# Eight weight subtracts of a hybrid encoder trunk placed on GpSimd instead of VectorE

## The chip, the cores and the metric

The kernel runs on one core of one Trainium2 chip. The metric is the device time of one execution in microseconds, median of three runs. A core has a matmul engine (TensorE, PE in the rows), a vector engine (VectorE, DVE), an activation engine (ScalarE, ACT), GpSimd (POOL) and SyncE (SP), which here issues every DMA. Each engine works through its own instructions in a fixed order; between engines there are only semaphore waits.

## What is computed

Two post-norm residual layers on 512 tokens of width 1024, in f32. Layer 0 mixes with windowed attention and a state-space model (S5), layer 1 with a matrix-memory LSTM (mLSTM); behind each mixer stand a residual add with a layer norm, a gated FFN with a depthwise convolution of three taps, and a second residual add with a norm.

```python
SEQ, D_MODEL, D_FF, DEPTH = 512, 1024, 2816, 2
for layer in range(DEPTH):
    y = attn_s5_mixer(x, ...) if layer % 2 == 0 else mlstm_mixer(x, ...)
    x = layer_norm(DEEPNORM_ALPHA * x + y, ln_g[layer, 0], ln_b[layer, 0])
    f = conv_ffn(x, ffn_w_up[layer], ffn_conv_w[layer], ffn_conv_b[layer], ffn_w_down[layer])
    x = layer_norm(DEEPNORM_ALPHA * x + f, ln_g[layer, 1], ln_b[layer, 1])

def conv_ffn(x, w_up, conv_w, conv_b, w_down):
    a, g = jnp.split(x @ w_up, 2, axis=-1)
    return (jax.nn.gelu(dwconv3(a, conv_w, conv_b)) * g) @ w_down

def layer_norm(x, g, b):
    mu = x.mean(-1, keepdims=True)
    var = jnp.mean(jnp.square(x - mu), -1, keepdims=True)
    return (x - mu) * lax.rsqrt(var + LN_EPS) * g + b
```

## The kernel before

**Products in two parts.** PE multiplies rounded f32 (fp32r). So each factor is split into a high part (the rounded value) and a low part (what rounding left), and a product is three matmuls: high by high, high by low, low by high (L545 to L547 in `mm3`, L569 in `nat_tile`).

**Weights in units.** All weights come as 192 units of 128x1024 f32, 512 KB each, in the order of their use. `load_unit` handles one: SP issues the DMA into a staging tile `st` (L511; two of them in the pool `wst`), ACT casts it to the high part `wh` (L528), and `wl = st - wh` is the low part (L529), formed on DVE, or on POOL for the units in the set `ON_POOL`. The subtract is the last reader of `st`, so the DMA of the unit two further on waits for it. `wh` and `wl` live in rings (3 tiles in ring A, 5 in ring B); `prefetch` and `get` set how many units are loaded ahead of their use. Units 14 to 16 serve the S5 gate and the first part of the layer-0 output projection, 17 to 19 the rest of it, 20 to 85 the first FFN (FFN0), 118 to 125 the layer-1 output projection, 126 to 191 the second FFN (FFN1).

**Around the start of an FFN.** The work there is the end of an output projection, four norms, and the first products of the FFN, all interleaved:

- `nat_last` goes over the four token tiles. For each it runs the last matmuls of the output projection (L569), then `norm` (`done`). Half way through tiles 2 and 3 PE also transposes tiles 0 and 1 of the normed residual `x` (`transposes`, L623).
- `norm` for one tile: two adds of the residual to the projection (L591, DVE, from PSUM), the mean (L606, DVE), the square (L607, ACT), `lny = (x - mean) * g` (L608, DVE, 128x1024), the variance (L609, DVE), its power -1/2 `lnrs` (L610, POOL, 128x1), and two halves of `x = lny * lnrs + b` (L613, DVE, 128x512 each).
- `transposes` for one tile: two times four matmuls against the identity (L623), a cast to `xh` (L627, ACT), and `xl` = transposed x minus `xh` (L628, DVE, from PSUM).
- `ffn` begins with three units in two halves of 256 token columns: the first half needs only tiles 0 and 1, and the transposes of tiles 2 and 3 stand between its matmuls.

**Ahead of FFN0** stands the S5 gate (`s_glu`): for each of four feature groups PE makes a bank, ACT a tanh `y` (L1234), DVE a product in `y` (L1236), ACT a cast `mh` (L1240), DVE its low part `ml` (L1241). The tile `x` of the residual is loaded by one DMA of 2 MB (L1332); its space was used by an input of the last `y` product, so that DMA waits for the last L1236. The first four units of FFN0 have the names `wl_2654` (unit 20), `wl_2660` (21), `wl_2865` (22), `wl_2871` (23); those of FFN1 are `wl_8019` (126), `wl_8025` (127), `wl_8249` (128), `wl_8255` (129).

**Order.** Up to the S5 gate the order on each engine is set by a planner with a table of biases; from there on, so at both places of this change, by the scheduler of the tile framework, which orders each engine's instructions by its own estimate of their times.

Of the kernel before, what the change touches and what calls it, by code (L numbers as in the profile page):

```python
# [50 lines left out]
_FFN = "AAA" + "BAB" * 20 + "BBB"  # L51
RINGS = "A" * 10 + "XXXX" + "AAA" + "BBB" + _FFN + "VV" + "A" * 30 + "AAA" + "BBBBB" + _FFN

ON_POOL = set(range(96, 118))

VG = 256 + 32

# [391 lines left out]
class Net:  # L449
# [54 lines left out]
    def load_unit(self, parts=None):  # L504
# [12 lines left out]
        hi, lo = parts  # L517
        pool = ENG_W[i] == "g" if self.plan else i in ON_POOL
        eng = nc.gpsimd if pool else nc.vector
# [1273 lines left out]
```

## Time and profile before

| what | value |
|---|---|
| runs | 1277.31, 1279.6 and 1280.5 us; median 1279.6 us |
| the profiled execution | 1281.08 us, its span in the trace 1279.3 us |
| granted PE clock, mean | 0.985 of full speed |
| PE busy | 1245.1 us, 97% of the span |
| DVE busy | 718.8 us, 56% |
| ACT busy | 527.8 us, 41% |
| POOL busy | 138.0 us, 11% |

The span runs from the first to the last record of the trace; the time of the execution is 1.78 us longer. A busy share is that of the whole span. A line of a timeline gives the start, the length, the engine, the line of code, the operation with its output and inputs, and in brackets how long the engine stood idle before it and what released it; neighbours of one kind are joined with a count.

### The profile page before, as it was taken

To read this page: it belongs to the slowest core of one execution; us is meant where nothing else is said; L and a number is where in the kernel's file an instruction comes from. 1 tells how busy PE (TensorE), PEld (TensorE's weight loads), DVE (VectorE), ACT (ScalarE), POOL (GpSimd) and SP (SyncE) were. 2 spreads that over 40 slices of the span, in tenths; PEclk is the share of its full clock that TensorE was granted. 3 is DMA by queue.
4 is the path that set the end of the run, shared out by engine and by line. 5 is a ranking of instruction groups with operands and counts; after the bars stand their busy time and mean duration, and the time that the engine had idled before them with its cause. 6 is when DMAs were issued, how large, how long until landed. Compare 5 with 4: busy or idle time off the path is not lost.

```text
span 1279.3 us, 17610 instructions
## 1 busy us (share of the span) xinstructions
PE 1245.1 (97%) x6878; PEld 1044.2 (82%) x6878; DVE 718.8 (56%) x1398; ACT 527.8 (41%) x900; POOL 138.0 (11%) x139
## 2 busy tenths in 40 slices
PE   7989899999999999999999999999999999999997
PEld 5777787788888888888889898988988888888886
DVE  7998984765442444434675747375864422544415
ACT  5346764353331233322365747453443321333301
POOL 2013520000000000000015344310000000000000
PEclk9988889999999999999999999999999999999999
DMA  8533633453332333323033232323343321433301
GB/s 249 177 112 98 179 104 110 151 167 99 99 99 85 95 117 98 92 72 101 26 117 99 83 99 75 91 66 132 125 139 99 99 90 60 148 99 97 91 27 66
DMA packets 57459, 135.31 MB, mean 106 GB/s; under 512 B 13888, under 2 KB 22928, under 8 KB 56736
## 3 DMA queue, kind: packets, MB, share of 16 engines
q1 hardware_dynamic: 57376, 134.19, 33.7%
q8 instruction: 54, 0.88, 0.3%
q14 instruction: 29, 0.24, 0.1%
HBM read 129.19 MB, written 4.98 MB: 105 GB/s over the span
## 4 chain that ended last, share of the span: by engine, by line
PE 82%; DVE 10%; DMA 4%; issue 3%; ACT 1%; SPq 0%; POOL 0%; DVEq 0%; POOLq 0%; ACTq 0%
PE b L569 22%; PE b L545 17%; PE b L546 17%; PE b L547 17%; PE b L446 3%; DVE t L446 2%; PE b L1557 1%; PE b L1555 1%; DMA zx<-DZ 1%; DMA t<-xT_dram 1%; DVE C L446 1%; DMA st<-w_dram 1%; DMA x<-x_dram 1%; DVE s L446 1%; DVE c L446 1%
## 5 line engine op out<-in xcount | busy, mean ns | idle before, releaser
L546 PE MATMUL b<-xl,wh 128*128 128x512 f32 (+1 forms) x944 | 357.3, 379 | 1.0 <-DVE xl L628 1.0
L545 PE MATMUL b<-xh,wh 128*128 128x512 f32 (+1 forms) x944 | 357.6, 380 | 0.5 <-ACT xh L627 0.5
L547 PE MATMUL b<-xh,wl 128*128 128x512 f32 (+1 forms) x944 | 357.0, 378 | 0.0
L528 ACT CAST wh<-st 128x1024 fp32r<-128x1024 f32 x175 | 183.7, 1051 | 413.3 <-DMA st<-w_dram 141.0
L529 DVE TENSOR_TENSOR wl<-st,wh 128x1024 fp32r<-128x1024 f32 x153 | 188.1, 1231 | 293.4 <-ACT wh L528 289.6
L546 PEld LDWEIGHTS b<-xl,wh 128*128 128x128 f32 x944 | 177.6, 188 | 34.8 <-DVE xl L628 2.1
L547 PEld LDWEIGHTS b<-xh,wl 128*128 128x128 f32 x944 | 177.6, 188 | 33.2
L545 PEld LDWEIGHTS b<-xh,wh 128*128 128x128 f32 x944 | 177.2, 188 | 33.4 <-ACT xh L627 1.0
L569 PE MATMUL b<-wh,hh 128*128 128x512 f32 x352 | 109.3, 390 | 0.0
L569 PE MATMUL b<-wh,hl 128*128 128x512 f32 x352 | 109.2, 389 | 0.0
L569 PE MATMUL b<-wl,hh 128*128 128x512 f32 x352 | 109.2, 389 | 0.0
L610 POOL TENSOR_TENSOR lnrs<-lnsq,mhalf 128x1 f32<-128x1 f32 x16 | 9.7, 604 | 836.1 <-DVE lnsq L609 774.2
L569 PEld LDWEIGHTS b<-wh,hl 128*128 128x128 f32 x352 | 66.1, 188 | 13.8
L569 PEld LDWEIGHTS b<-wl,hh 128*128 128x128 f32 x352 | 66.1, 188 | 13.7
L569 PEld LDWEIGHTS b<-wh,hh 128*128 128x128 f32 x352 | 65.9, 188 | 13.6
L734 DVE TENSOR_TENSOR c<-c,b 128x512 f32<-128x512 f32 x44 | 30.2, 687 | 65.8 <-PE b L547 65.0
L733 ACT ACTIVATE c<-c 128x512 f32<-128x512 f32 x44 | 27.8, 632 | 80.9 <-DVE c L732 80.8
L529 POOL TENSOR_TENSOR wl<-st,wh 128x1024 fp32r<-128x1024 f32 x22 | 52.4, 2388 | 54.2 <-ACT wh L528 51.3
L591 DVE SCALAR_TENSOR_TENSOR x<-x,b 128x512 f32<-128x512 f32 x48 | 31.1, 683 | 43.0 <-PE b L569 39.3
L446 PE MATMUL b<-xh,wh 128*128 128x512 f32 x80 | 33.1, 418 | 8.1 <-ACT xh L446 8.1
L607 ACT ACTIVATE lnjk<-x,lnmu 128x1024 f32<-128x1024 f32 x16 | 18.5, 1154 | 51.0 <-DVE lnmu L606 51.0
L446 ACT ACTIVATE s<-s,m 128x384 f32<-128x384 f32 (+3 forms) x64 | 33.7, 557 | 13.7 <-DVE m L446 13.4
(330 smaller groups left out, 1864.0 us busy)
## 6 DMA issues: line engine op xcount, KB each, us to landing
st<-w_dram SPq DMA_DIRECT2D x192, 512.0 KB, 3.6
tb<-s5bT_dram SPq DMA_DIRECT2D x16, 256.0 KB, 4.4
zx<-DZ SPq DMA_DIRECT2D x16, 256.0 KB, 4.9
lngb<-ln_dram SPq DMA_DIRECT2D x4, 1024.0 KB, 4.7
nb<-DN SPq DMA_DIRECT2D x16, 256.0 KB, 3.5
t<-xT_dram SPq DMA_DIRECT2D x8, 256.0 KB, 5.7
T<-DK SPq DMA_DIRECT2D x32, 64.0 KB, 2.2
x<-x_dram SPq DMA_DIRECT2D x1, 2048.0 KB
```

The source lines that it names most:

```text
L446: getattr(getattr(nc, s.eng), s.name)(*real(s.args), **real(s.kw))
L528: nc.scalar.copy(out=h, in_=x)
L529: eng.tensor_tensor(out=l, in0=x, in1=h.bitcast(F32), op=ALU.subtract)
L545: mm(ps, lhsT=lh, rhs=rh, start=first, stop=False)
L546: mm(ps, lhsT=lh, rhs=rl, start=False, stop=False)
L547: mm(ps, lhsT=ll, rhs=rh, start=False, stop=last)
L569: mm(acc[h], lhsT=hx[:, tok], rhs=wx[:, 512 * h:512 * h + 512], start=a, stop=b)
L591: self.nc.vector.scalar_tensor_tensor(out=xr, in0=xr, scalar=scale, in1=acc[h], op0=ALU.mult, op1=ALU.add, **kw)
L607: nc.scalar.activation(out=jk, in_=x, func=AF.Square, bias=mu, accum_out=sq)
L733: nc.scalar.activation(out=c, in_=c, func=AF.Gelu_apprx_tanh)
L734: nc.vector.tensor_tensor(out=c, in0=c, in1=pg, op=ALU.mult)
L1555: nc.tensor.matmul(pn[:, 0:130], lhsT=Ws[j][:, i - j, :], rhs=va[:, j, h % 2, 0:130], start=j == 0, stop=j == i)
```

## The change

The set of the units whose low part is formed on POOL gets the first four units of each FFN. Nothing else is edited.

```diff
-ON_POOL = set(range(96, 118))
+ON_POOL = set(range(96, 118)) | {20, 21, 22, 23, 126, 127, 128, 129}
```

The scheduler orders the engines anew, and three places are to be seen. In the rows below a name is that of the code with a number for the tile, and the brackets hold the semaphores that an instruction waits for.

**The start of FFN0.** SP, from the weight DMA of unit 21 on; `st_2862` and `st_2868` are units 22 and 23, `st_2874` and `st_3065` units 24 and 25, `x_2622` is the residual, `lngb` the norm's constants:

```order
 L511 DMA st_2657<-w_dram 128x1024 [waits DMAHW7_49,DMAHW5_49,DVE_49]
-L511 DMA st_2862<-w_dram 128x1024 [waits DMAHW6_49,DMAHW0_49,DVE_49]
-L511 DMA st_2868<-w_dram 128x1024 [waits DMAHW7_49,DVE_49]
+L511 DMA st_2862<-w_dram 128x1024 [waits DMAHW6_49,DMAHW0_49,Pool_49]
+L511 DMA st_2868<-w_dram 128x1024 [waits DMAHW7_49,Pool_49]
 L1332 DMA x_2622<-x_dram 128x4096 [waits DMAHW2_49,DVE_49,PE_49]
-L584 DMA lngb_2631<-ln_dram 128x2048 [waits Pool_49]
+L584 DMA lngb_2631<-ln_dram 128x2048
-L511 DMA st_2874<-w_dram 128x1024 [waits DMAHW4_49,DMAHW1_49,DVE_49]
-L511 DMA st_3065<-w_dram 128x1024 [waits DMAHW0_49,DVE_49]
+L511 DMA st_2874<-w_dram 128x1024 [waits DMAHW4_49,DMAHW1_49,Pool_49]
+L511 DMA st_3065<-w_dram 128x1024 [waits DMAHW0_49,Pool_49]
```

The order of these DMAs is as it was; four weight DMAs now wait for POOL instead of DVE, and the load of `x` stands behind two of them. On POOL the four subtracts stand among the powers of the norms:

```order
+L529 TENSOR_TENSOR wl_2654<-st_2651,wh_2653 128x1024 [waits DMAHW6_49,PE_49,Activation_49]
+L529 TENSOR_TENSOR wl_2660<-st_2657,wh_2659 128x1024 [waits PE_49,DMAHW7_49,Activation_49,Pool_49]
+L529 TENSOR_TENSOR wl_2871<-st_2868,wh_2870 128x1024 [waits DMAHW1_49,DVE_49,Activation_49]
+L610 TENSOR_TENSOR lnrs_2690<-lnsq_2689,mhalf_74 128x1 [waits DVE_49,Pool_49]
 L610 TENSOR_TENSOR lnrs_2729<-lnsq_2728,mhalf_74 128x1 [waits DVE_49]
+L529 TENSOR_TENSOR wl_2865<-st_2862,wh_2864 128x1024 [waits DMAHW0_49,Activation_49,Pool_49]
 L610 TENSOR_TENSOR lnrs_2782<-lnsq_2781,mhalf_74 128x1 [waits DVE_49,Pool_49]
```

Three of them are ahead of the power of tile 0, and unit 22 stands between the powers of tiles 1 and 2.

**The norm of tile 2, ahead of the first products of FFN0.** DVE; `lny_2784` belongs to tile 2, `xl_83` is the low part of the transposed x, here of the two halves of tile 1:

```order
 L606 TENSOR_SCALAR lnmu_2780<-lnsm_2779 128x1
 L608 SCALAR_TENSOR_TENSOR lny_2784<-x_2622,lnmu_2780,lngb_2631 128x1024
-L529 TENSOR_TENSOR wl_2865<-st_2862,wh_2864 128x1024
 L609 TENSOR_SCALAR lnsq_2781<-lnsq_2781 128x1
+L613 SCALAR_TENSOR_TENSOR x_2622<-lny_2784,lnrs_2782,lngb_2631 128x512 x2
 L628 TENSOR_TENSOR xl_83<-b_2806,xh_82 128x4x128
-L613 SCALAR_TENSOR_TENSOR x_2622<-lny_2784,lnrs_2782,lngb_2631 128x512 x2
 L628 TENSOR_TENSOR xl_83<-b_2813,xh_82 128x4x128
```

The subtract of unit 22 is gone from DVE, and both halves of tile 2's L613 have moved ahead of the first low part of tile 1.

**The start of FFN1.** POOL; `hrs_7882` is the last power of the mLSTM, `lnrs_8061` and `lnrs_8106` belong to the norms of tiles 0 and 1:

```order
 L1582 TENSOR_TENSOR hrs_7882<-hrs_7882,mhalf_74 128x4 [waits DVE_49,Pool_49]
+L529 TENSOR_TENSOR wl_8019<-st_8016,wh_8018 128x1024 [waits DMAHW2_49,Activation_49]
 L610 TENSOR_TENSOR lnrs_8061<-lnsq_8060,mhalf_74 128x1 [waits DVE_49]
+L529 TENSOR_TENSOR wl_8025<-st_8022,wh_8024 128x1024 [waits DMAHW3_49,Activation_49]
+L529 TENSOR_TENSOR wl_8249<-st_8246,wh_8248 128x1024 [waits DMAHW4_49,Activation_49,Pool_49]
 L610 TENSOR_TENSOR lnrs_8106<-lnsq_8105,mhalf_74 128x1 [waits DVE_49]
+L529 TENSOR_TENSOR wl_8255<-st_8252,wh_8254 128x1024 [waits DMAHW5_49,Activation_49,Pool_49]
```

Unit 126 stands ahead of the power of tile 0, units 127 and 128 right behind it. On DVE the same stretch reads:

```order
 L591 SCALAR_TENSOR_TENSOR x_2622,lnsm_8103<-x_2622,b_7906 128x512
-L529 TENSOR_TENSOR wl_8025<-st_8022,wh_8024 128x1024
 L613 SCALAR_TENSOR_TENSOR x_2622<-lny_8063,lnrs_8061,lngb_7952 128x512 x2
 L606 TENSOR_SCALAR lnmu_8104<-lnsm_8103 128x1
-L529 TENSOR_TENSOR wl_8249<-st_8246,wh_8248 128x1024
 L608 SCALAR_TENSOR_TENSOR lny_8108<-x_2622,lnmu_8104,lngb_7952 128x1024
```

The two subtracts around tile 0's L613 are gone from DVE, and L613 follows the last add of tile 1.

## Rows read from the trace of the kernel before

**Rows 1.** Two stretches: length, busy PE, PEld, DVE, ACT, POOL; clock, DMA, GB/s

```profile
185.00:275.00 90.00, 87.81 (x638) 74.91 (x635) 56.91 (x86) 41.50 (x60) 3.13 (x4) 1.00 0.39 130
880.00:930.00 50.00, 49.76 (x303) 44.16 (x302) 37.03 (x59) 24.29 (x32) 2.18 (x4) 1.00 0.43 140
```

**Rows 2.** Waits of PE, 190 to 275 us: total us, times, longest

```profile
PE b L546 <- DVE xl L628: 1.0, 3, 0.4
...
PE b L569 <- ACT y L1234: 0.3, 1, 0.3
```

**Rows 3.** All instructions of line L529: ns min/median/max, first and last start

```profile
L529 DVE TENSOR_TENSOR wl<-st,wh x153: 1215/1225/2300, 207.9 to 1243.6; 128x1024 fp32r<-128x1024 f32 x153
...
L529 POOL TENSOR_TENSOR wl<-st,wh x22: 2349/2396/2411, 670.1 to 832.4; 128x1024 fp32r<-128x1024 f32 x22
```

**Rows 4.** Timeline of DVE, then of POOL, about 670 us

```profile
670.59 2.48 DVE L1505 TENSOR_TENSOR kl<-c,kh 128x512 fp32r<-128x512 f32 x1 [1.06 <-ACT kh L1504]
...
670.12 2.40 POOL L529 TENSOR_TENSOR wl<-st,wh 128x1024 fp32r<-128x1024 f32 x1 [4.56 <-ACT wh L528]
```

**Rows 5.** Timeline of POOL, then of DVE, about 700 us

```profile
700.16 1.02 POOL L1582 TENSOR_TENSOR hrs<-hrs,mhalf 128x4 f32<-128x4 f32 x1
701.15 2.35 POOL L529 TENSOR_TENSOR wl<-st,wh 128x1024 fp32r<-128x1024 f32 x1
...
701.22 3.13 DVE L1584 TENSOR_SCALAR hn<-hn,hmv,hrs 128x128 f32<-128x128 f32 x4 [1.14 <-POOL hrs L1582]
```

**Rows 6.** Timeline of POOL, then of DVE, about 150 us

```profile
149.47 1.79 POOL L446 TENSOR_TENSOR C<-C,c 128x512 f32<-128x512 f32 x1
...
149.46 0.67 DVE L446 TENSOR_TENSOR ra<-ra,rb 128x512 f32<-128x512 f32 x1
150.05 2.29 DVE L446 TENSOR_TENSOR_SCAN rb<-R,ra 128x512 f32<-128x512 f32 x1
```

**Rows 7.** Start of FFN0, timeline of DVE, then SP, PE, ACT

```profile
218.38 0.69 DVE L1236 SCALAR_TENSOR_TENSOR y<-y,s 128x512 f32<-128x512 f32 x1
...
225.37 0.69 DVE L1236 SCALAR_TENSOR_TENSOR y<-y,t 128x512 f32<-128x512 f32 x1
...
235.47 0.69 DVE L591 SCALAR_TENSOR_TENSOR x<-x,b 128x512 f32<-128x512 f32 x1 [3.76 <-DMA x<-x_dram]
...
248.80 1.28 DVE L608 SCALAR_TENSOR_TENSOR lny<-x,lnmu,lngb 128x1024 f32<-128x1024 f32 x1
...
252.02 1.42 DVE L613 SCALAR_TENSOR_TENSOR x<-lny,lnrs,lngb 128x512 f32<-128x512 f32 x2
...
226.12 1.45 SPq L1332 DMA_DIRECT2D x<-x_dram  x1
...
241.14 1.22 PE L623 MATMUL b<-ident,x 128*128 128x128 f32 x8
...
251.94 0.39 PE L546 MATMUL b<-xl,wh 128*128 128x256 f32 x1 [0.40 <-DVE xl L628]
...
246.49 1.06 ACT L528 CAST wh<-st 128x1024 fp32r<-128x1024 f32 x1 [1.69 <-PE b L569]
```

**Rows 8.** Start of FFN1, timeline of DVE, then POOL and PE

```profile
895.37 1.22 DVE L529 TENSOR_TENSOR wl<-st,wh 128x1024 fp32r<-128x1024 f32 x1
896.51 1.41 DVE L613 SCALAR_TENSOR_TENSOR x<-lny,lnrs,lngb 128x512 f32<-128x512 f32 x2
...
894.93 0.55 POOL L610 TENSOR_TENSOR lnrs<-lnsq,mhalf 128x1 f32<-128x1 f32 x1 [23.82 <-DVE lnsq L609]
...
896.99 0.62 PE L569 MATMUL b<-wh,mh 128*128 128x512 f32 x2
897.45 1.18 PE L623 MATMUL b<-ident,x 128*128 128x128 f32 x8
```

**Rows 9.** Same columns as rows 1, early in the kernel

```profile
46.00:48.00 2.00, 1.10 (x30) 0.99 (x32) 2.00 (x10) 0.96 (x4) 0.00 (x0) 1.00 0.56 115
48.00:54.00 6.00, 5.80 (x34) 4.57 (x31) 5.30 (x20) 0.44 (x1) 0.00 (x0) 0.72 0.74 254
```

## The prediction

> **What bounds the kernel now.** I read first how much of each stretch PE is busy, then what PE waits for there, then the engines' timelines around those waits. PE bounds the kernel: in the stretch around the start of FFN0 it is busy for 87.81 of 90 us, around the start of FFN1 for 49.76 of 50, at full granted clock in both [rows 1]. What it waits for at the start of FFN0 is little: 1.0 us in three waits for `xl`, which DVE makes, and 0.3 us for the tanh of the gate [rows 2]; at FFN1 all idle time is 0.24 us [rows 1]. So all that a relief of DVE can win there is 1.0 + 0.3 + 0.24, about 1.5 us of 1280. The question is what the change may lose: DVE is not spread thin there, it makes the norm that PE's transposes wait for.
>
> **What the edit moves.** Eight subtracts leave DVE, where one takes 1.225 us, and go to POOL, where the same form takes 2.396 [rows 3]: 9.8 us less on DVE, 19.2 us more on POOL, neither of which bounds the kernel over the span. As a count of busy time that costs nothing. Two things give it a price.
>
> First, POOL and DVE hinder each other. A DVE subtract of 128x512 with both inputs in SBUF that begins 0.47 us into a POOL subtract lasts 2.48 us and ends 0.55 us after it [rows 4]; a product of that size and kind takes 0.69 us where POOL is idle (L1236 at 218.38) [rows 7]. So DVE stood still for the rest of the POOL instruction. Second, a POOL subtract that is queued behind a power goes ahead of the DVE work that the power releases: the power ends at 701.18, the subtract begins at 701.15, and DVE's L1584, released by that power, stands 3.13 us for four pieces and ends 0.85 us after the subtract [rows 5]. And where both have work, they take turns: POOL's add at 149.47 waits for DVE's `ra`, then holds up the scan that stands right behind `ra` on DVE, 2.29 us long [rows 6]. Which DVE instructions are exposed follows from the code: L1236, L1241, L608, L613 and L529 read two SBUF operands; L591 and L628 read one from PSUM and I take them as free.
>
> The Trainium skill, Perfetto Trace Analysis, section "Optimizing Scalar/DVE Operations", speaks for such an offload where DVE is saturated and against one between DVE and GpSimd, since these share a port and it "might not help". By its first half the change would win at most the 1.5 us above; rows 4 and 5 side with the second, and the steps below price it.
>
> **Start of FFN0, units 20 and 21: +1.9 us.** Subtract 20 stood on DVE right ahead of the product L1236 at 218.38 [rows 7]. On POOL it begins at about 217.3 and ends at 219.7; the L1236 now stands ahead of it in DVE's queue but is held until 219.65, +1.13 us net. The rest of the gate is a chain DVE, ACT, DVE, so it carries this on. Subtract 21 then runs on POOL from about 225.4 to 227.8 and holds up the last L1236, which ran from 225.37 to 226.06 [rows 7], and would end at 228.4: +2.35. Behind that wait on SP stands the 2 MB load of `x`, issued at 226.12 [rows 7], in the same breath as the weight DMA ahead of it, which now waits for POOL. So the load is issued 2.3 us later. DVE waited 3.76 us for just this load, until 235.47 [rows 7], so nothing hides it. Some comes back, since the next weight DMA (unit 24) also goes later and shares the load's last microseconds less: I take 2.0. PE's transposes of tile 0 stand at 241.14, 1.22 us long for eight [rows 7], right behind the L613 that feeds them, so PE has no slack there: 1.9 us, of which 1.1 show already at the gate. Bounds: 0.8 (the gate's delay hidden by the load's queue, half the load's delay made up) to 2.4.
>
> **Start of FFN0, units 22 and 23: +1.6 us.** Unit 23 falls into the wait for `x`: nothing. Unit 22's cast stands at 246.49 [rows 7], with the shift at 248.4, so its POOL subtract covers about 249.5 to 251.9. L608 of tile 2 stood at 248.80 [rows 7], would be ready at 250.7, and is held until 251.9. From there: 1.28 for L608 (253.2), 0.7 for variance and power (a power alone takes 0.55 [rows 8]; 253.9), 1.42 for L613 of tile 2, which has moved ahead of L628, then 0.68 for L628: `xl` is there at about 255.9. Before, PE's first matmul with it stood at 251.94, after a wait of 0.40 [rows 7]. With PE going on at 256.0 the total shift is 4.1 us; less the other two waits for `xl`, 0.6 us together [rows 2], which fall away since what they wait for now comes sooner after: 3.5, so 1.6 beyond the 1.9. Bounds: 0 (subtract 22 finds L608 already running and DVE's own saving of 1.225 pays for the order) to 2.2.
>
> **Start of FFN1: +3.9 us.** Subtract 126 stood ahead of the first adds of the norm; without its 1.225 us [rows 3] these start up to that much earlier, but then its POOL form holds up L608 for about as long: the power of tile 0 comes 0.2 us earlier, no more. The power of tile 0 stands at 894.93, subtract 127 at 895.37, L613 behind it at 896.51, the transposes at 897.45 [rows 8]. In the new order subtracts 127 and 128 are queued on POOL right behind that power, as in rows 5. The power ends at 895.28, subtract 127 takes 895.25 to 897.6, the first half of L613 897.6 to 898.3, then by turns [rows 6] subtract 128 to 900.6 and the second half of L613 to 901.3. PE reaches the transposes at 896.99 (they stand ahead of these two matmuls now [rows 8]), waits 1.36 for the first four, makes them, and waits 2.55 for the other four: 3.9 us. No wait of before stands behind it that could give anything back [rows 1]. Bounds: 1.6 if either half of L613 goes ahead of the subtract beside it; 3.9 above. I take the upper end, since its order is that of rows 5 and 6.
>
> The Trainium skill, SBUF — State Buffer, section "Who interferes with whom", has the port as a lock held for a whole instruction, by whoever issues first. By that rule too subtract 127 has the port before L613 can ask, and this term is 3.9 and not 1.6; rows 5 agree, since the released L1584 waited.
>
> **The clock: +1.6 us.** PE idles 3.9 of 4.4 us there. In the stretch from 46 to 48 us it was busy for 1.10 of 2 us, and in the 6 us from 48 on the mean granted clock was 0.72 of full speed, that is, it stood on the lower of its two levels for a part of them [rows 9]. With 5.80 busy us in them that cost 5.80 x 0.28 = 1.6 us. I count one such fall, after the wait at FFN1. Bounds: 0 (no fall) to 3.2 (a second one at FFN0, where the idling comes in several pieces).
>
> **Sum.** 1.9 + 1.6 + 3.9 + 1.6 = 9.0 us. The profiled execution took 1281.08 us (1279.3 span and 1.78 around it), 1.5 above the median of the runs; by its own time the sum gives 1290.1, by the median 1288.6. I forecast **1288.6**. Ends of all bounds: 0.8 + 0 + 1.6 + 0 = 2.4 and 2.4 + 2.2 + 3.9 + 3.2 = 11.7, so 1282.0 and 1291.3. About 0.3% (3.8 us) is what a measurement of this kernel can tell from no change.
>
> **Rivals.**
> - *The delays hide (about 1281).* Subtracts and norm fall between each other, because the scheduler's order makes the cast come late or the engines slip past each other; one of the places survives with its lower bound (1.6). For it: half of the terms hang on offsets of under 1 us between a cast and a norm. Against: DVE works nearly without a gap there and the subtracts on POOL stand directly behind what DVE waits for. 26%.
> - *DVE's relief shows (about 1278).* The subtracts find gaps in DVE's exposed work; then DVE's norm chain is 1.2 us shorter per unit, and PE's waits for `xl` and the gate go. This is the other side: it decides at L613 of FFN1, if its halves run before POOL takes up subtract 127, which needs the cast of unit 127 to end 0.1 us or more after the power instead of before it. Its price is bounded by PE's idle time, 1.5 us: 1278.1. It stays within 0.3%. 5%.
> - *The clock falls twice or stays down longer (about 1291).* Both places make PE idle; the sum with 3.2 for the clock and the upper end of the load's delay, 2.4 for 1.9, is 11.1: 1290.7. 17%.
> - *The change doesn't do what it says.* The order shows the eight subtracts on POOL; nothing else hangs on the set. Under 1%, no time of its own.
>
> **Chances.** The forecast, from 1284 to 1289.5: 52%. With the rivals: faster by over 0.3% has 2% (no row carries it; PE has no more than 1.5 us to win), within 0.3% 29% (the first two rivals), slower by over 0.3% 69%. For 8 in 10 the range leaves out the relief and a part of the hidden case below, and what lies over two clock falls above: 1280.8 to 1291.5.
>
> **What would show it.** In the profile after: DVE's L1236 around 218 and 228 us with 2 us and more instead of 0.69; the issue of `x` at about 228.4 and its landing at 237 to 238; a wait of PE for `xl` of 2 us or more near 255; L613 of tile 0 in FFN1 with 4 to 6 us for its two halves instead of 1.41, and PE's transposes there with two waits of 1.4 and 2.5 us; a granted clock under 1.00 behind them. I am wrong if L613 keeps 1.4 us there (POOL took the port later), if `x` lands as before (the load has slack that I don't see), or if the lengths grow but PE's waits don't.

## The result: slower by 0.64%

The changed kernel takes 1288.61 us in the median of five runs (1284.74 to 1289.44); the kernel before, timed beside it, 1277.31 us (1275.93 to 1280.5). The measured ratio is 1.0064 with a 95% interval of 1.0046 to 1.0081, that is +8.2 us (+5.9 to +10.3). The two medians lie further apart, 11.3 us; medians of five runs are that loose, and those of the kernel before in the later measurements, of 26 to 31 runs, are 1279.1 to 1279.6 us. Forecast were 1288.6 us and +9.0.

To see where the time went I divide the span by four instructions that both kernels have: the first tanh of the S5 gate (L1234 on ACT), the first residual add that ends the first half of FFN0 (L591), the last tile's first add in the last norm of FFN0 (L591), and the first residual add that ends the first half of FFN1. Timelines of ACT and DVE, kernel before:

```profile
213.53 0.60 ACT L1234 ACTIVATE y<-b 128x512 f32<-128x512 f32 x1 [4.69 <-PE b L547]
...
415.40 0.69 DVE L591 SCALAR_TENSOR_TENSOR x<-x,b 128x512 f32<-128x512 f32 x1 [0.97 <-PE b L569]
...
617.11 0.69 DVE L591 SCALAR_TENSOR_TENSOR x<-x,b 128x512 f32<-128x512 f32 x1 [0.28 <-PE b L569]
...
1070.92 0.69 DVE L591 SCALAR_TENSOR_TENSOR x<-x,b 128x512 f32<-128x512 f32 x1 [1.04 <-PE b L569]
```

The same four of the kernel after:

```profile
210.31 0.60 ACT L1234 ACTIVATE y<-b 128x512 f32<-128x512 f32 x1 [4.51 <-PE b L547]
...
417.48 0.69 DVE L591 SCALAR_TENSOR_TENSOR x<-x,b 128x512 f32<-128x512 f32 x1 [1.05 <-PE b L569]
...
619.19 0.69 DVE L591 SCALAR_TENSOR_TENSOR x<-x,b 128x512 f32<-128x512 f32 x1 [0.28 <-PE b L569]
...
1078.10 0.69 DVE L591 SCALAR_TENSOR_TENSOR x<-x,b 128x512 f32<-128x512 f32 x1 [0.66 <-PE b L569]
```

The first stretch ("FFN0 stretch" below) takes 201.87 us before and 207.17 after, +5.30. The second takes 201.71 in both. The third ("FFN1 stretch") takes 453.81 and 458.91, +5.10. What lies ahead of the gate was 3.22 us shorter in this execution of the kernel after, and the rest of the span is equal: 5.30 + 5.10 - 3.22 = 7.2, the difference of the two spans (1286.5 and 1279.3). The 3.22 is not the change's: nothing is moved ahead of the gate, and the twelve further profiles below have it between 0.06 and 5.32 us earlier than the kernel before.

The same two stretches as in [rows 1], kernel after (length, busy PE, PEld, DVE, ACT, POOL, granted clock, DMA share, GB/s):

```profile
185.00:275.00 90.00, 84.33 (x536) 71.39 (x535) 52.25 (x75) 36.97 (x54) 12.71 (x8) 0.98 0.37 125
880.00:930.00 50.00, 46.46 (x258) 39.99 (x257) 32.88 (x50) 18.29 (x25) 11.96 (x8) 0.97 0.43 137
```

PE is idle for 5.67 us in the first (2.19 before) and 3.54 in the second (0.24 before), and the mean clock, 1.00 before, is below it in both. What PE waited for, 190 to 275 us (answers [rows 2]):

```profile
PE b L546 <- DVE xl L628: 2.4, 1, 2.4
PE b L623 <- DVE x L613: 1.5, 1, 1.5
PE b L569 <- ACT y L1234: 0.9, 1, 0.9
```

and 880 to 930 us:

```profile
PE b L623 <- DVE x L613: 3.3, 2, 2.1
```

**Start of FFN1.** Timeline of the kernel after, POOL, then DVE, then PE (answers [rows 8]):

```profile
892.66 2.41 POOL L529 TENSOR_TENSOR wl<-st,wh 128x1024 fp32r<-128x1024 f32 x1 [19.50 <-ACT wh L528]
896.90 0.55 POOL L610 TENSOR_TENSOR lnrs<-lnsq,mhalf 128x1 f32<-128x1 f32 x1 [1.83 <-DVE lnsq L609]
897.41 2.39 POOL L529 TENSOR_TENSOR wl<-st,wh 128x1024 fp32r<-128x1024 f32 x1
900.06 2.49 POOL L529 TENSOR_TENSOR wl<-st,wh 128x1024 fp32r<-128x1024 f32 x1 [0.26 <-ACT wh L528]
...
893.28 0.68 DVE L591 SCALAR_TENSOR_TENSOR x<-x,b 128x512 f32<-128x512 f32 x1
...
897.49 5.62 DVE L613 SCALAR_TENSOR_TENSOR x<-lny,lnrs,lngb 128x512 f32<-128x512 f32 x2
...
900.41 0.66 PE L623 MATMUL b<-ident,x 128*128 128x128 f32 x4 [1.21 <-DVE x L613]
903.16 1.11 PE L623 MATMUL b<-ident,x 128*128 128x128 f32 x4 [2.10 <-DVE x L613]
```

The power of tile 0 ends at 897.45. The subtract of unit 127 is already begun (897.41), and the L613 that the power released stands for 5.62 us instead of 1.41: its first half until the subtract has ended, its second behind unit 128's. This hold is not a semaphore wait: it ties the two engines together although neither waits for a result of the other. PE's transposes wait twice, 1.21 and 2.10 us. L591, which reads one operand from PSUM, keeps its 0.68 us inside the POOL subtract at 892.66. The Trainium skill, SBUF — State Buffer, section "Who interferes with whom", says that a vector instruction with at most one SBUF input, outside the two-port modes, does not contend with GpSimd; the 0.68 agrees.

**Start of FFN0.** DVE, then SP, POOL and PE (answers [rows 7]):

```profile
214.38 2.50 DVE L1236 SCALAR_TENSOR_TENSOR y<-y,s 128x512 f32<-128x512 f32 x1 [0.27 <-ACT y L1234]
...
222.44 2.55 DVE L1236 SCALAR_TENSOR_TENSOR y<-y,t 128x512 f32<-128x512 f32 x1 [0.36 <-ACT y L1234]
...
235.08 0.69 DVE L591 SCALAR_TENSOR_TENSOR x<-x,b 128x512 f32<-128x512 f32 x1 [7.82 <-DMA x<-x_dram]
...
248.95 1.74 DVE L608 SCALAR_TENSOR_TENSOR lny<-x,lnmu,lngb 128x1024 f32<-128x1024 f32 x1
...
251.48 1.42 DVE L613 SCALAR_TENSOR_TENSOR x<-lny,lnrs,lngb 128x512 f32<-128x512 f32 x2 [0.73 <-POOL lnrs L610]
...
225.04 0.33 SPq L1332 DMA_DIRECT2D x<-x_dram  x1
...
247.22 2.39 POOL L529 TENSOR_TENSOR wl<-st,wh 128x1024 fp32r<-128x1024 f32 x1 [2.41 <-issue]
...
240.58 1.32 PE L623 MATMUL b<-ident,x 128*128 128x128 f32 x8 [1.47 <-DVE x L613]
...
253.55 0.39 PE L546 MATMUL b<-xl,wh 128*128 128x256 f32 x1 [2.37 <-DVE xl L628]
```

The two gate products that meet a POOL subtract take 2.50 and 2.55 us instead of 0.69. The load of `x` is issued 14.73 us behind the first tanh (12.59 before), `x` is there at 24.77 (21.94), PE waits 1.47 us for tile 0's L613, where it had no wait, and 2.37 us for `xl`.

**The clock.** Granted clock (the 0.77, 0.50 and so on ahead of the last two columns) behind the two long waits, kernel after:

```profile
253.00:255.00 2.00, 1.45 (x9) 1.45 (x10) 2.00 (x5) 1.25 (x2) 0.00 (x0) 0.77 0.04 12
255.00:257.00 2.00, 2.00 (x11) 2.00 (x11) 2.00 (x6) 0.32 (x1) 0.00 (x0) 0.50 0.00 0
257.00:259.00 2.00, 2.00 (x17) 2.00 (x17) 1.27 (x3) 1.39 (x3) 0.55 (x1) 0.87 0.65 195
901.00:903.00 2.00, 0.07 (x1) 0.00 (x0) 2.00 (x1) 0.00 (x0) 1.56 (x1) 0.91 0.65 244
903.00:905.00 2.00, 1.84 (x7) 1.64 (x8) 1.67 (x4) 1.67 (x4) 0.16 (x1) 0.50 0.65 162
905.00:907.00 2.00, 2.00 (x8) 1.63 (x7) 1.57 (x3) 0.53 (x2) 0.39 (x1) 0.74 0.28 109
```

Both times the clock falls to the lower of its two levels, 0.50. The share lost over each six us is 2 x (0.23 + 0.50 + 0.13) = 1.7 us and 2 x (0.09 + 0.50 + 0.26) = 1.7 us, a little less where PE idled in them. With PE's added idle time that is the whole of both stretches between these two profiles: 5.67 - 2.19 + 1.7 = 5.2 (measured +5.30), and 3.54 - 0.24 + 1.7 = 5.0 (measured +5.10). How much of the 5.30 belongs to the change is another matter: 2.8 us of it is a later landing of `x`, which varies by itself (below).

### The profile page after: what moved, and what is told of

The parts are those of the page before. It is cut to its first block, busy times and chain, and to the rows that moved or that the text cites. A ratio compares the mean times of both kernels' runs of the same rounds, so it can differ in the third digit from the quotient of the medians.

```text
span 1286.5 us, 17612 instructions
## 1 busy us (share of the span) xinstructions
PE 1244.7 (97%) x6878; PEld 1043.6 (81%) x6878; DVE 715.5 (56%) x1390; ACT 526.8 (41%) x900; POOL 161.2 (13%) x147
## 4 chain that ended last, share of the span: by engine, by line
PE 82%; DVE 8%; DMA 4%; issue 2%; ACT 2%; SPq 1%; POOL 0%; DVEq 0%; POOLq 0%; ACTq 0%
PE b L569 20%; PE b L545 18%; PE b L546 18%; PE b L547 18%; PE b L446 4%; PE b L1557 1%; PE b L1555 1%; DVE t L446 1%; DMA st<-w_dram 1%; SPq L446 1%; DMA zx<-DZ 1%; DMA t<-xT_dram 1%; DVE x L613 1%; DMA x<-x_dram 1%; DVE C L446 1%
## 5 line engine op out<-in xcount | busy, mean ns | idle before, releaser
L529 DVE TENSOR_TENSOR wl<-st,wh 128x1024 fp32r<-128x1024 f32 x145 | 177.2, 1224 | 291.4 <-ACT wh L528 287.9
L529 POOL TENSOR_TENSOR wl<-st,wh 128x1024 fp32r<-128x1024 f32 x30 | 71.9, 2401 | 130.4 <-ACT wh L528 122.9
L591 DVE SCALAR_TENSOR_TENSOR x<-x,b 128x512 f32<-128x512 f32 x48 | 31.1, 682 | 48.9 <-PE b L569 41.0
```

What stands on the lines that cost most here:

```text
L529: eng.tensor_tensor(out=l, in0=x, in1=h.bitcast(F32), op=ALU.subtract)
L591: self.nc.vector.scalar_tensor_tensor(out=xr, in0=xr, scalar=scale, in1=acc[h], op0=ALU.mult, op1=ALU.add, **kw)
```

## Experiments

Theory: a POOL subtract holds back DVE instructions that read two SBUF operands, for its whole length; where PE waits for these instructions (two places), PE idles and its clock falls. Rivals: the weights' low parts come later from the slower engine and that delays PE or the staging tiles; the scheduler's new order costs, not POOL; the load of `x`, issued later, is (or is not) one of the causes. All kernels are the kernel before with the edit shown, timed in three rounds beside it. The stretches are those from above, of one profiled execution each; the last column is the landing of `x`, read as the start of the first L591 behind the first tanh.

| kernel | FFN0 stretch, us | FFN1 stretch, us | ratio to before (95% interval) | landing of `x`, us |
|---|---|---|---|---|
| before | 201.87 | 453.81 | | 21.94 |
| after, first profile | 207.17 | 458.91 | 1.0064 (1.0046 to 1.0081) | 24.77 |
| after, once more | 204.57 | 458.85 | 1.0059 (1.0038 to 1.0080) | 23.67 |
| units 20 to 23 | 203.73 | 454.30 | 1.0029 (1.0012 to 1.0047) | 22.63 |
| units 126 to 129 | 202.71 | 458.57 | 1.0047 (1.0030 to 1.0063) | 22.53 |
| eight units in mid FFN | 202.92 | 453.83 | 1.0002 (0.9983 to 1.0021) | 23.06 |
| eight subtracts left out | 203.41 | 453.63 | 0.9981 (0.9962 to 1.0000) | 21.30 |
| units 20, 21 | 203.31 | 453.79 | 1.0001 (0.9985 to 1.0017) | 22.67 |
| unit 22 | 204.07 | 454.04 | 1.0011 (0.9998 to 1.0024) | 23.10 |
| unit 22's subtract left out | 201.40 | 453.89 | 1.0003 (0.9988 to 1.0018) | 21.33 |
| idle subtracts on POOL | 203.76 | 458.68 | 1.0044 (1.0029 to 1.0060) | 23.76 |
| idle memsets on POOL | 203.07 | 453.78 | 0.9999 (0.9986 to 1.0012) | 23.08 |
| unit 127 | 202.89 | 456.50 | 1.0023 (1.0007 to 1.0040) | 22.87 |
| units 23, 126, 129 | 202.81 | 455.24 | 1.0014 (1.0002 to 1.0025) | 22.89 |

How exact a stretch is shows in the kernels that change nothing in it. The FFN1 stretch lies between 453.63 and 454.30 in the eight whose POOL does at the start of FFN1 what it did before. The FFN0 stretch is looser: in six kernels with nothing changed at its start (before, units 126 to 129, mid FFN, both idle ones, unit 127) it is 201.87 to 203.76, and the profile of before is the lowest of them; the middle is 202.9. This spread is that of the landing of `x`: from 21.94 to 23.76 us behind the tanh the stretch grows by 1.89 us for 1.82 of landing and in the same order.

### One place at a time

```diff
-ON_POOL = set(range(96, 118))
+ON_POOL = set(range(96, 118)) | {20, 21, 22, 23}
```

> Only units 20 to 23 on POOL. Theory (POOL's subtracts hold up DVE's two-operand work, PE then waits and its clock falls): the stretch from the gate to the mid FFN0 is longer than before by what it is in the changed kernel, 5.3 us (3.5 us more waits of PE and a clock fall of 1.6 to 1.8), the second FFN as before; total about +5 us. Rival (the eight longer subtracts delay the weights, wherever they stand): half of the whole, about +4 to +5, but spread evenly, without PE waits for the norm. Rival (both places hinder each other): less or more than half, no sum.

```diff
-ON_POOL = set(range(96, 118))
+ON_POOL = set(range(96, 118)) | {126, 127, 128, 129}
```

> Only units 126 to 129 on POOL. Theory: FFN0 as before; the two halves of tile 0's L613 in FFN1 stand 5.6 us instead of 1.4, PE waits 3.3 us for them and loses 1.6 to 1.8 to its clock: +5.1 us. Rival (later weights): no wait of PE for L613.

Both places cost, and each its own. FFN1 alone: stretch +4.76, L613 at 5.62 us for its two halves as in the whole change, PE waiting 2.8 us for it; ratio 1.0047, +6.0 us. FFN0 alone: ratio 1.0029, +3.7 us; the two together would be 9.7, the whole change measured 8.2 and 7.5; within their intervals they add. But the profile of FFN0 alone does not have the expected 5.3: its stretch is +1.85, PE waits 0.9 us for the gate and 2.5 for `xl` as in the kernel after, 0 for L613, and the clock stays at 1.00. Two parts of the 5.3 are thus not there every time.

### The same amount elsewhere, and not at all

```diff
-ON_POOL = set(range(96, 118))
+ON_POOL = set(range(96, 118)) | {40, 41, 42, 43, 146, 147, 148, 149}
```

> Eight other units, 40 to 43 and 146 to 149, in the middle of both FFNs, on POOL instead. Theory: PE never waits for DVE there, so the same amount of POOL time costs nothing: within 0.3%, -1 to +1 us. Rival (later weights: each subtract 1.17 us longer, and the staging tiles free later): about the +8 to +10 us of the change. Rival (any POOL subtract beside DVE work costs): several us.

Eight subtracts more on POOL in the middle of the FFNs cost nothing that can be measured (1.0002; FFN1 stretch +0.02). That speaks against "slower subtracts delay the weights" and against "any POOL subtract costs": it is the place.

```diff
-        hi, lo = parts
+        hi, lo = parts; lo = hi if i in GONE else lo
...
-            eng.tensor_tensor(out=l, in0=x, in1=h.bitcast(F32), op=ALU.subtract)
+            i in GONE or eng.tensor_tensor(out=l, in0=x, in1=h.bitcast(F32), op=ALU.subtract)
```

with GONE = {20, 21, 22, 23, 126, 127, 128, 129}; the high part of these units stands in for their low part:

> The eight subtracts are left out on DVE and on POOL; the high part of those units is used in place of their low part. What relief of DVE is worth when nothing is put on POOL: theory: PE's waits around the norms bound it, at most 1.5 us faster, within 0.3%; at tile 2 of FFN0 the new order (L613 ahead of L628) may still cost some of it. Rival (DVE's norm chain is what these stretches hang on): 1.2 us for each subtract in a norm, 5 us and more faster.

This is what the change could have won if POOL were free of charge: 0.19% (0 to 0.38%), about 2.4 us, not to be told from none. In its profile the FFN1 stretch is 0.18 us shorter, no more than its spread. Its FFN0 stretch is 0.5 us over the middle, with a fall of the clock in it. The time taken off DVE was not what bounded either stretch.

### Is it the port, or the later weights?

At FFN1 all subtracts go back to the engines of before; POOL does two more that nobody waits for, with ALSO = {127, 128}.

```diff
+    def also(self, i, h):
+        if i in ALSO:
+            self.nc.gpsimd.tensor_tensor(out=self.scr, in0=h.bitcast(F32), in1=h.bitcast(F32), op=ALU.subtract)
...
-            eng.tensor_tensor(out=l, in0=x, in1=h.bitcast(F32), op=ALU.subtract)
+            eng.tensor_tensor(out=l, in0=x, in1=h.bitcast(F32), op=ALU.subtract); self.also(i, h)
...
-        self.open_late()
+        self.open_late(); self.scr = self.t(self.open("scr"), [P, 1024], "scr")
```

> All subtracts on the engines of before; POOL also forms two subtracts of 128x1024 that nobody waits for (the high part minus itself, into a tile that is not read), right behind the power of tile 0 in FFN1, when units 127 and 128 are cast. Theory (the shared port): DVE's L613 there is held by them though nothing hangs on their result: 4 us or more for its two halves, PE waits 2.5 to 5 us, +3 to +6.5 us with the clock. Rival (what costs is that the weights' low parts come later from POOL): as before, within 0.5 us in the FFN1 stretch.

Timeline of that kernel, POOL, DVE, PE:

```profile
892.02 5.20 POOL L1689 TENSOR_TENSOR scr<-wh 128x1024 f32<-128x1024 f32 x2
...
893.09 4.68 DVE L613 SCALAR_TENSOR_TENSOR x<-lny,lnrs,lngb 128x512 f32<-128x512 f32 x2
...
895.52 0.66 PE L623 MATMUL b<-ident,x 128*128 128x128 f32 x4 [1.34 <-DVE x L613]
897.82 0.81 PE L623 MATMUL b<-ident,x 128*128 128x128 f32 x4 [1.64 <-DVE x L613]
```

The FFN1 stretch is +4.87 us although no instruction hangs on these results, no weight's low part comes from POOL and DVE's own order is that of before. PE's only added wait from 880 to 930 us is the 3.0 us for L613, and the clock falls as in the kernel after (mean 0.97). That settles it for FFN1: POOL's subtracts hold L613 back, and PE with it.

The counterpart should have put POOL work that reads nothing at the same place:

```diff
+    def also(self, i, h):
+        for _ in range(2 if i in ALSO else 0):
+            self.nc.gpsimd.memset(self.scr, 0.0)
```

> As the run with two idle subtracts, but POOL writes zeros (two memsets of 128x1024 each time, no input) instead. Theory (the port for reading, held by an instruction that reads two tiles): L613 1.4 to 1.5 us, the FFN1 stretch as before within 0.5 us. Rival (POOL busy in any way holds DVE, or delays the powers queued behind): L613 3 us or longer, or the power of tile 1 late by 1 us or more and PE waiting.

It tells nothing on L613. The memsets wait for no input, so the scheduler put them far ahead; all instructions of that line (ns min/median/max, first and last start):

```profile
L1689 POOL MEMSET scr<- x4: 954/955/958, 856.5 to 859.5; 128x1024 f32 x4
```

They ran 30 us before the norm, and FFN1 is unchanged (stretch -0.03). But the last of them meets another DVE instruction with two SBUF operands, the product L1595:

```profile
859.50 0.68 DVE L1595 SCALAR_TENSOR_TENSOR hx<-og,hx 128x512 f32<-128x512 f32 x1
```

The memset runs from 859.50 for 0.96 us, over the whole of it, and L1595 keeps the 0.68 us that it has in the kernel before, where POOL is idle then. So POOL work that reads nothing did not hold such a product; with L613 itself it was not tried.

### One subtract behind the power

```diff
-ON_POOL = set(range(96, 118))
+ON_POOL = set(range(96, 118)) | {127}
```

> Unit 127 alone on POOL, queued right behind the power of tile 0 in FFN1. Theory: the first half of L613 is held for the subtract's 2.4 us, the second follows at once: L613 3.7 to 3.9 us for both, PE waits 1 to 1.7 us in one piece and its clock stays: +1.2 to +1.8 us in the FFN1 stretch, a third of the four units' 4.8 to 5.1. Rival (the whole is one event that any of the units sets off): +4 us or more.

DVE and PE of that kernel:

```profile
892.17 3.52 DVE L613 SCALAR_TENSOR_TENSOR x<-lny,lnrs,lngb 128x512 f32<-128x512 f32 x2
...
895.08 1.32 PE L623 MATMUL b<-ident,x 128*128 128x128 f32 x8 [1.39 <-DVE x L613]
```

With one subtract queued there L613 is held once (3.52 us) and PE waits once, 1.39 us; the clock stays at 1.00. The stretch is +2.69, more than the 1.2 to 1.8 expected. PE waits another 0.7 us for a later `xl`; with the 1.39 that is 2.1, just what L613 was held (3.52 less 1.41), so the delay of DVE came to PE whole, in two parts. The other 0.6 us were not traced. So the 4.8 to 5.1 of the four units are about two such holds and the fall of the clock, which one hold alone did not bring.

### Unit 22: hold or order?

In the kernel after L608 of tile 2 was held for only 0.46 us (1.74 for 1.28), yet PE waited 2.37 us for `xl`. Two kernels part the hold from the order. The first:

```diff
-ON_POOL = set(range(96, 118))
+ON_POOL = set(range(96, 118)) | {22}
```

> Only unit 22 on POOL; on DVE tile 2's L613 stands ahead of tile 1's L628, as in the changed kernel. Theory A (POOL holds up L608, as predicted): L608 1.7 us or longer, PE's waits for xl 1 us or more above before. Theory B (the new order does it: L628 waits for the power and for L613): the same wait of PE, but L608 held for under 0.5 us; L628 late by 0.7 for the power and 1.3 for L613. In both +1 to +2.5 us, with a clock fall up to +4.

The second has the edit of the kernel without the eight subtracts, with GONE = {22}; its DVE order in the norm of tile 2 is the same, tile 2's L613 ahead of tile 1's L628:

> Unit 22's subtract left out on both engines (its high part is used as its low part), DVE's order as with unit 22 on POOL. Theory B (order): PE still waits about 1 to 2 us for xl at the first products of FFN0, as before plus most of what unit 22 on POOL costs. Theory A (the hold of POOL): L608 at 1.28 us and no added wait: as before or up to 0.5 us faster.

Unit 22 on POOL (POOL, DVE, PE):

```profile
246.20 2.39 POOL L529 TENSOR_TENSOR wl<-st,wh 128x1024 fp32r<-128x1024 f32 x1 [3.02 <-issue]
...
247.32 2.35 DVE L608 SCALAR_TENSOR_TENSOR lny<-x,lnmu,lngb 128x1024 f32<-128x1024 f32 x1
...
252.53 0.39 PE L546 MATMUL b<-xl,wh 128*128 128x256 f32 x1 [2.47 <-DVE xl L628]
```

Unit 22's subtract left out (DVE, PE):

```profile
245.09 1.28 DVE L608 SCALAR_TENSOR_TENSOR lny<-x,lnmu,lngb 128x1024 f32<-128x1024 f32 x1
...
247.33 1.42 DVE L613 SCALAR_TENSOR_TENSOR x<-lny,lnrs,lngb 128x512 f32<-128x512 f32 x2 [0.73 <-POOL lnrs L610]
...
249.40 0.39 PE L546 MATMUL b<-xl,wh 128*128 128x256 f32 x1 [1.15 <-DVE xl L628]
```

From L608's start to PE's matmul it is 3.14 us in the kernel before (248.80 to 251.94 [rows 7]), 4.31 with the new order and no subtract, 5.21 with unit 22 on POOL, 4.60 in the kernel after. So the order alone makes `xl` 1.17 us later, although a subtract of 1.22 us has left DVE: L628 now stands behind a power that DVE waits 0.73 us for, and behind L613's 1.42. The hold adds 0.9 when POOL's subtract falls fully on L608, and 0.3 in the kernel after. Both theories are right, and in the kernel after the order is the larger part. That holds for the time at which `xl` is there; by whole times neither kernel can be told from before (1.0011 and 1.0003).

### The gate and the load of `x`

```diff
-ON_POOL = set(range(96, 118))
+ON_POOL = set(range(96, 118)) | {20, 21}
```

> Only units 20 and 21 on POOL. Theory as predicted: L1236 at 2.5 us twice, the load of x issued 2 us later, PE waits 0.6 us more for the gate and 0.8 to 1.6 for tile 0's L613: +1.9 us. Rival (the load's landing does not follow its issue one for one; its spread hides the delay): 0.9 us wait for the gate, no more than the usual spread of 0 to 1.6 us for L613: +0.6 us, within 0.3%.

> The changed kernel once more. In the first profile the load of x landed late (PE waited 1.5 us for tile 0's L613 in FFN0) and the clock fell there too. Theory (that wait belongs to the load's own spread, which kernels with an unchanged gate show as well, and not to the gate's delay): the FFN0 stretch comes out anywhere from +1.9 to +5.5 us against the profile of before, the FFN1 stretch again +4.5 to +5.3; the ratio again about 1.005 to 1.008. Rival (the gate's delay makes it): a wait of 1 us or more for L613 in FFN0 again.

For units 20 and 21 alone the rival was right on the load. PE waits 0.9 us for the gate instead of 0.3, in this kernel and in the three others with these units on POOL, and 1.7 us for `xl` instead of 1.0; the stretch is 0.4 us over the middle of the unchanged ones (0.5 over what those beside its landing of `x` have: 202.71 at 22.53 and 202.89 at 22.87), and the ratio 1.0001. L1236 stands at 2.5 us twice and the load of `x` is issued 2.1 us later, as forecast, but:

```profile
236.14 0.69 DVE L591 SCALAR_TENSOR_TENSOR x<-x,b 128x512 f32<-128x512 f32 x1 [2.58 <-DMA x<-x_dram]
```

This is 22.7 us behind the first tanh of that kernel. In nine kernels whose gate is that of before, this distance is 21.3 to 23.8 us (21.94 in the profile of before, 22.9 in the middle); in the four with units 20 and 21 on POOL it is 22.6, 22.7, 23.7 and 24.8. The load's own spread is as large as the delay of its issue, and PE waits for tile 0's L613 in seven of the nine as well (0.3 to 1.6 us). Why the landing does not follow the issue was not traced.

The longer wait for `xl` has its own cause, a fourth change of DVE's order that is not among the three shown at the start. In the kernel before tile 0's L613 stands between the two adds of tile 1; with units 20 and 21 on POOL it stands ahead of both, and DVE waits for its power:

```profile
240.83 1.41 DVE L613 SCALAR_TENSOR_TENSOR x<-lny,lnrs,lngb 128x512 f32<-128x512 f32 x2 [0.45 <-POOL lnrs L610]
```

From the landing of `x` to PE's first matmul with `xl` it is 16.5 us in all six unchanged kernels, 17.0 here, 17.6 with unit 22's subtract left out, 18.2 with all eight left out, and 18.5 to 18.7 with unit 22 on POOL (18.5 in both profiles of the kernel after). With the eight left out DVE's order is that of the kernel after and POOL holds nothing. So of the 2.0 us by which `xl` comes later there, 1.7 are the order's.

The changed kernel once more, waits of PE from 190 to 275 us, and the stretch of [rows 1]:

```profile
PE b L546 <- DVE xl L628: 2.4, 1, 2.4
PE b L569 <- ACT y L1234: 0.9, 1, 0.9
...
PE b L623 <- DVE x L613: 0.4, 1, 0.4
...
185.00:275.00 90.00, 85.35 (x546) 71.95 (x545) 53.78 (x79) 38.37 (x54) 12.71 (x8) 1.00 0.39 132
```

The gate's 0.9 and the 2.4 for `xl` are there again, the wait for L613 is 0.4 instead of 1.5, and the clock did not fall: +2.70 instead of +5.30. `x` landed 1.1 us earlier than in the first profile. The FFN1 stretch repeats (+5.04).

### The three subtracts that should cost nothing

```diff
-ON_POOL = set(range(96, 118))
+ON_POOL = set(range(96, 118)) | {23, 126, 129}
```

> Units 23, 126 and 129 alone on POOL, the three whose subtracts were predicted to cost nothing. Theory: FFN1 stretch within 0.5 us of before, FFN0 as in kernels unchanged there; ratio within 0.3%. Rival (each POOL subtract costs about a microsecond wherever it stands): +3 us.

Not quite: the ratio is 1.0014, inside the 0.3% expected, but the FFN1 stretch is +1.43, not within 0.5 us. Unit 129's subtract meets L608 of tile 2 (POOL, DVE), and PE waits 1.1 us for an `xl`:

```profile
900.82 2.39 POOL L529 TENSOR_TENSOR wl<-st,wh 128x1024 fp32r<-128x1024 f32 x1 [2.88 <-issue]
...
901.48 2.81 DVE L608 SCALAR_TENSOR_TENSOR lny<-x,lnmu,lngb 128x1024 f32<-128x1024 f32 x1
```

In the kernel after this wait is not there: the same L608 begins at 909.53 and unit 129's subtract at 910.51, behind it.

## Why the prediction was right, point by point

**What bounds the kernel, and the relief: borne out.** By PE's waits at the two places the gain was to be 1.5 us at most; without the eight subtracts on either engine the kernel is 0.19% faster, 2.4 us with both 0 and 1.5 inside the interval.

**FFN1, +3.9 us: right in mechanism, 0.6 too high.** POOL takes up unit 127 behind the power, L613 is held half by half (5.62 us; the forecast had it from 895.3 to 901.3, 6.0), PE waits twice. The waits were 1.21 and 2.10 us for forecast 1.36 and 2.55. The choice between 3.9 and the lower bound of 1.6 hung on turns between the engines, and POOL had its turn between the halves of L613. Idle subtracts showed that nothing but the hold is needed.

**The clock, +1.6: right for one fall** (1.7 by the windows). The second fall, left to a rival, came in the first profile of the kernel after (1.7 at FFN0) and not in the second.

**FFN0, units 20 and 21, +1.9: wrong in its main part.** The step that failed is the one from the issue of the load to its landing: "So the load is issued 2.3 us later", "so nothing hides it", taken as 2.0. The issue was 2.1 us later, as forecast, but `x` landed 22.6 to 24.8 us behind the gate's start instead of 21.3 to 23.8, a shift of 0.3 us between the middles (22.9 and 23.2) and of 0.7 between the means (22.7 and 23.4), within a spread of 2.4; four profiles don't size it better. I had read one execution's landing as a fixed time; the profile of before happened to have an early one. The step behind it, "PE has no slack there", held: in the unchanged kernels a later landing lengthens the stretch one for one. What is left of the term is the gate's 0.6 us, below its lower bound of 0.8, and what part of the shift is real. That the order which goes with these two units also brings `xl` 0.5 us later was not in the forecast.

**FFN0, units 22 and 23, +1.6: inside its bounds, but the split was wrong.** I had L608 held 1.2 us by the POOL subtract. It was held 0.46; the rest comes from L613 standing ahead of L628, which the forecast had in its sum but beside the hold. By L608 to PE's matmul it is +1.46 us, where the forecast had 2.2, and the two smaller waits for `xl`, 0.6 us, fell away as said: 0.9 us is left of the 1.6.

**Sum.** 3.5 for FFN0 against +0.8 to +4.3 over the middle of the unchanged kernels in three profiles (+3.7 by the ratio of units 20 to 23); 5.5 for FFN1 with its clock against 4.8 to 5.1. That the median met the forecast to 0.1 us is luck in part: one term was too high by about 1.3, and a second clock fall and late landings of `x` in some executions make up for it. Measured again, the same kernel has a median of 1286.85 us and a ratio of 1.0059. The FFN0 part stays loosely sized: units 20 and 21 alone and unit 22 alone add up to 1.5 us by their ratios, units 20 to 23 together have 3.7 (1.5 to 6.0).

**The rivals.** That the delays hide is out: FFN1 alone is slower by 0.47%. "The clock falls twice" is one of the executions seen.

## What to carry to other kernels

Before work goes from VectorE to GpSimd, look for VectorE instructions with two SBUF inputs that a bounding engine waits for: in these runs a GpSimd subtract queued right behind the short GpSimd operation that releases them went ahead of them, and they stood for its whole length. These are not the only ones: L1584 of [rows 5], which reads one tile and two columns of factors, was held as well (2.36 us for the first piece, median 0.34). Eight subtracts of the same size cost nothing measurable where the bounding engine waits for no such instruction. And an instruction taken off an engine lets a scheduler reorder what is left: look in the new order for what now stands ahead of the value that is waited for, and size a DMA's landing from more than one execution.

## What was not expected of the hardware

The clock did not follow one long wait. At FFN0 PE waited 2.4 to 2.5 us in one piece for `xl` in the kernel after and again in its second profile, with units 20 to 23 and with unit 22 alone; only in the first of these four did the granted clock fall, there with 1.47 us of waiting 11 us ahead. The kernel with the eight subtracts left out fell too (mean clock 0.98 from 185 to 275 us) after a wait of 2.1. At FFN1, with 2.8 to 3.3 us in two pieces, it fell in all four profiles that have them. And the load of 2 MB spread over 2.4 us in its landing with the gate ahead of it unchanged.
